# Fixing the order of GpSimd's instructions in the heads' stage of a hybrid attention layer

## The chip, the cores and the metric

The kernel runs on one core of a Trainium2 chip. The metric is device microseconds of one execution. The profile is of one execution apart from the timed ones; its instructions and transfers come from the hardware profiler.

## What is computed

One decoder layer in float32 on 512 tokens of width 2048. Two branches read the same normalised input: sliding-window attention with sinks, and a gated DeltaNet with 16 key heads and 32 value heads of width 128. They are gated, merged and projected. The change touches the DeltaNet branch, whose core is this (cut):

```python
g = jnp.cumsum(g, axis=-1)
decay = jnp.exp(jnp.where(tril, g[..., :, None] - g[..., None, :], -jnp.inf))
...
qk = jnp.where(tril, jnp.einsum('bhncd,bhnsd->bhncs', q, k) * decay, 0.0)
q_dec = q * jnp.exp(g)[..., None]
...
def step(S, xs):
    u_c, w_c, qk_c, qd_c, kd_c, gl_c = xs
    v_new = u_c - w_c @ S
    o = qd_c @ S + qk_c @ v_new
    S = S * gl_c[..., None, None] + jnp.swapaxes(kd_c, -1, -2) @ v_new
    return S, o
```

The layer ends with `y_b = o @ w_o_dn` and a last projection by `w_out`. Both are done by seven products of half-sized blocks each (m1 to m7) in place of eight, for which sums of blocks of the weights are needed.

## The kernel before

Every large product takes three float32r matmuls (L245 to L247): each operand is split into a high part, a cast on ScalarE (`whi`, L52), and a low part, a subtraction on VectorE (`wlo`, L53). Weights come in 1 MB tiles on SyncE's queue (L205).

`deltanet` first makes keys and a triangular inverse, then runs the heads' stage: 16 groups, each with one key head and its two value heads (e = 0, 1). For a group, `heads` runs five channel tiles on TensorE (queries, values 0, values 1, two gates), 48 matmuls each. Beside them, generators (`queries`, `values`, `zgate`, `scan`) are stepped by `pump`, eight times a tile: they issue the small work of this group and the rest of the last one. I call the stretch from a group's sum of squares of queries (L769) to the next group's the segment of that group.

In `queries`, GpSimd and ScalarE work like this for each head:

- `decay_load` (L774) has a row of cumulated gates put on all partitions, into a tile `E`. There are four such tiles, so two groups' worth.
- `decay_mask`, on GpSimd: L781 subtracts the gates of the other axis, L782 (an affine select) masks the upper triangle.
- L926, on ScalarE, takes the exponential; L938, on VectorE, multiplies it with query-key products; the scan's matmul L1004 reads it.
- L932, on GpSimd, multiplies the queries `yq` with decays loaded into `qe`; the scan's L1003 reads that.

In `values`, the convolution goes over ScalarE (L582, `yv`), VectorE (L586, three times), ScalarE again (tanh, L591) and VectorE (L593); TensorE transposes the result (L279, `ptv`) and ScalarE copies it (L882). On VectorE there stand between these: L900 (four columns, for the queries), L1035 and L1042 (output of the group before) and L1051 to L1054 (`head_sums`, sums of its halves, stored by SyncE in L1057). In group 5's segment ScalarE also copies the second inverse out (L836), which SyncE stores (L840).

Beside all this `quad_sums` makes the sums of blocks of `w_od`: a copy from one place of HBM to another (L701, SyncE's queue) and, four steps later, a transfer that adds another block to the copy (L704, GpSimd's queue, 32 of 1 MB). `od_sums` starts in group 2, and each step of `pump` advances it by 0.13 of a copy or transfer. In the attention stage `weight_sums` does the same for `w_out`.

Who goes first on an engine is decided by a scheduler that lists the instructions by when it expects them to be ready; program order counts only where a dependence ties. `behind` adds such ties without a semaphore: what is issued within it is listed after the last matmul so far. The transfers of `od_sums` are issued within it, by `ordered`; the masks, the products with queries and the exponentials of the heads' stage are not.

Of the kernel before, what the change touches and what calls it, by code (L numbers as in the profile page):

```python
# [11 lines left out]
ALU = mybir.AluOpType  # L12
# [4 lines left out]
P = 128  # L17
# [3 lines left out]
NTB = T // P  # L21
# [5 lines left out]
NEG = -1e30  # L27
# [9 lines left out]
class Layer:  # L37
# [66 lines left out]
    @contextmanager  # L104
    def behind(self):

        n, last = len(self.nc.cur_bb.bb.instructions), self.last_mm
        yield
        for i in self.nc.cur_bb.bb.instructions[n:]:
            self.tc.add_manual_dep(  # L110
                i, last.name, mybir.DependencyInfo(mybir.DependencyClass.NoSync, mybir.DependencyReason.DATA),
                reason="behind",
            )

    def step(self, e):
        try:
            e[1] = next(e[0]) or 1
        except StopIteration:
            self.live.remove(e)
# [162 lines left out]
    def build(self):  # L282
        tc, nc, a = self.tc, self.nc, self.a
        with ExitStack() as es:
            self.const = es.enter_context(tc.tile_pool(name="const", bufs=1))
            self.dram = es.enter_context(tc.tile_pool(name="scratch", bufs=1, space=DRAM))
            self.dnc_es = ExitStack()
            self.dnc = self.dnc_es.enter_context(tc.tile_pool(name="dnc", bufs=1, side="right"))
            self.v_d = self.dram.tile([2, P, T], F32, name="v_d")
            self.hpool = es.enter_context(tc.tile_pool(name="h", bufs=1))  # L290
            hh = self.hh = self.hpool.tile([P, KT, T], F32R, name="hh")
            hl = self.hl = self.hpool.tile([P, KT, T], F32R, name="hl")
            self.wraw = es.enter_context(tc.tile_pool(name="wraw", bufs=2, reuse_waits="tile"))
            self.whl = es.enter_context(tc.tile_pool(name="whl", bufs=3, reuse_waits="tile"))
            self.side, self.live, self.slow = {}, [], []
            self.hold, self.keep_order = 0, False
            self.od_d = {n: self.dram.tile([8, P, 2048], F32, name=f"od_{n}") for n in ("m7", "m5", "m6", "m4")}
            self.plan()
            self.psc_es = ExitStack()
            self.psc = self.psc_es.enter_context(tc.tile_pool(name="psc", bufs=4, space=PSUM, reuse_waits="tile"))  # L300
            with ExitStack() as st:
                self.startup(st)
            if self.stop == "startup":
                return
            self.ma_d = self.dram.tile([KT, P, T], F32, name="ma_d")
            self.mb_d = self.dram.tile([KT, P, T], F32, name="mb_d")
            self.ao_d = self.dram.tile([KT, P, T], F32, name="ao_d")
            self.yb_d = self.dram.tile([KT, P, T], F32, name="yb_d")
            self.gate_d = self.dram.tile([D], F32, name="gate_d")
            self.deltanet()  # L310
            self.psc_es.close()
            self.dnc_es.close()
            if self.stop == "deltanet":
                return
            self.y_d = self.dram.tile([KT, P, T], F32, name="y_d")
            self.branch_b()
            if self.stop == "branch_b":
                return
            self.attention()
            if self.stop == "attention":  # L320
                return
            self.finish()
# [369 lines left out]
    def quad_sums(self, q, d, lag):  # L692

        nc = self.nc
        n = len(q(0, 0))
        zip2 = lambda a, b: [x for p in zip(a, b) for x in p]
        copies = zip2(zip(d["m7"], q(1, 0)), zip(d["m5"], q(0, 0))) + list(zip(d["m6"], d["m7"])) + list(zip(d["m4"], d["m6"]))
        adds = zip2(zip(d["m7"], q(1, 1)), zip(d["m5"], q(1, 0))) + list(zip(d["m6"], q(0, 0))) + list(zip(d["m4"], q(0, 1)))
        for i in range(4 * n + lag):
            if i < 4 * n:  # L700
                nc.sync.dma_start(out=copies[i][0], in_=copies[i][1], max_dma_last_dim=8192)  # L701
                yield
            if i >= lag:
                nc.gpsimd.dma_start(out=adds[i - lag][0], in_=adds[i - lag][1], accum_op=ALU.add, max_dma_last_dim=8192)  # L704
                yield

    def weight_sums(self):
# [69 lines left out]
    def decay_mask(self, E, h):  # L777

        nc = self.nc
        ng = self.neg_g[:, :, h].unsqueeze(2).to_broadcast([P, NTB, P])  # L780
        nc.gpsimd.tensor_tensor(out=E, in0=E, in1=ng, op=ALU.add)  # L781
        nc.gpsimd.affine_select(  # L782
            out=E, in_=E, pattern=[[0, NTB], [1, P]], compare_op=ALU.is_ge, fill=NEG, base=0, channel_multiplier=-1
        )

    def solve_load(self, wk, b):
# [98 lines left out]
    def queries(self, wk, g, ps, st):  # L885

        nc = self.nc
        sl = lambda c: slice(c * P, (c + 1) * P)
        q = wk.tile([P, T], F32, tag="y", name="yq", bufs=3)
# [39 lines left out]
        yield 1  # L929
        for e in range(2):  # L930
            qf = qd[e].rearrange("p c i -> p (c i)")
            nc.gpsimd.tensor_tensor(out=qf, in0=qf, in1=q, op=ALU.mult)  # L932
        yield 1
        pqk = self.ptp.tile([P, NTB, P], F32, tag="tp", name="pqk")
        for c in range(NTB):
# [16 lines left out]
        for e in range(2):  # L952
            nc.vector.tensor_tensor(
                out=TT[e][0:HD, :, HD:P],
                in0=pu[e][0:HD],
                in1=self.neg_beta[0:HD, :, 2 * g + e].unsqueeze(2).to_broadcast([HD, NTB, HD]),
                op=ALU.mult,
# [761 lines left out]
```

## Time and profile before

| | |
|---|---|
| median of three timed runs | 2913.67 us (2909.84 to 2913.86) |
| profiled execution | 2902.22 us, its span 2900.5 us |
| TensorE busy | 2833.8 us (98%) |
| VectorE busy | 1863.0 us (64%) |
| ScalarE busy | 1141.2 us (39%) |
| GpSimd busy | 273.9 us (9%), 266 instructions |
| granted TensorE clock | 0.996 on average |
| heads' stage | from about 540 to 1660 us |

A row of the timeline has the start and the length in us, the engine, the line, what is written from what, and in brackets how long the engine stood idle before and what released it. A length includes any time in which the instruction was held up after its start. A row of the table by stage has the stretch, its length, then for TensorE, its weight loads, VectorE, ScalarE and GpSimd the busy time and (x) the instructions, then the granted clock, the share of DMA time and GB/s.

### The profile page before, as it was taken

How to read it: one execution, taken by the hardware profiler on the slowest of the kernel's cores; microseconds unless marked ns; L12 is line 12 of the kernel's file. 1: busy time of each engine (PE TensorE's matmuls, PEld its weight loads, DVE VectorE, ACT ScalarE, POOL GpSimd, SP SyncE). 2: the span in 40 equal slices, each digit the busy share in tenths (PEclk: the TensorE clock that was granted, in tenths of full speed). 3: DMA queues.
4: the chain of work that ended last, by engine and by line, in shares of the span. 5: the costliest groups of instructions: out<-in, count | busy, mean ns of one | idle time of the engine just before them, and what ended most of it. 6: DMA issues, size and time to landing. Idle time of an engine off the chain costs nothing.

```text
span 2900.5 us, 38269 instructions
## 1 busy us (share of the span) xinstructions
PE 2833.8 (98%) x14428; PEld 2322.5 (80%) x14428; DVE 1863.0 (64%) x3020; ACT 1141.2 (39%) x2161; POOL 273.9 (9%) x266
## 2 busy tenths in 40 slices
PE   8899999999999999999999999999999999999999
PEld 6677888888888888787777888888887788788777
DVE  6765998778776656665665456665556655554565
ACT  4355333433334333333333354443344434432343
POOL 0022211101111111111020000000100100000010
PEclk9999999999999999999999999999999999999999
DMA  9757554646667778777782377675745648365575
GB/s 386 288 163 216 161 180 148 203 130 203 204 189 218 235 204 258 227 238 229 226 219 94 133 254 264 241 255 202 223 147 162 171 143 225 112 240 177 182 235 153
DMA packets 205472, 590.08 MB, mean 203 GB/s; under 512 B 74564, under 2 KB 99652, under 8 KB 154088
## 3 DMA queue, kind: packets, MB, share of 16 engines
q1 hardware_dynamic: 195080, 529.44, 53.7%
q0 software_dynamic: 10208, 58.20, 10.2%
q8 instruction: 113, 1.85, 0.3%
q14 instruction: 71, 0.58, 0.1%
HBM read 523.79 MB, written 166.40 MB: 238 GB/s over the span
## 4 chain that ended last, share of the span: by engine, by line
PE 81%; issue 4%; DVE 4%; DMA 2%; POOL 1%; ACT 1%; SPq 0%; POOLq 0%; DVEq 0%; ACTq 0%
PE mm L245 19%; PE mm L247 18%; PE mm L246 18%; PE od L245 4%; PE od L246 4%; PE od L247 4%; PE m L246 1%; PE m L247 1%; PE m L245 1%; PE S L1356 1%; PE pv L985 1%; PE O L1407 1%; PE po L1004 1%; PE pP L279 1%; DVE wlo L53 1%
## 5 line engine op out<-in xcount | busy, mean ns | idle before, releaser
L245 PE MATMUL mm<-hh,whi 128*128 128x512 f32 x2784 | 1134.0, 407 | 2.3 <-ACT whi L52 1.6
L247 PE MATMUL mm<-hh,wlo 128*128 128x512 f32 x2784 | 1090.3, 392 | 1.1 <-DVE wlo L53 1.1
L246 PE MATMUL mm<-hl,whi 128*128 128x512 f32 x2784 | 1088.4, 391 | 0.0
L53 DVE TENSOR_TENSOR wlo<-raw,whi 128x1024 fp32r<-128x1024 f32 (+1 forms) x476 | 587.8, 1238 | 422.7 <-ACT whi L52 414.9
L52 ACT CAST whi<-raw 128x1024 fp32r<-128x1024 f32 (+1 forms) x476 | 495.5, 1044 | 777.8 <-PE mm L246 660.7
L247 PEld LDWEIGHTS mm<-hh,wlo 128*128 128x128 f32 x2784 | 523.2, 188 | 115.4 <-DVE wlo L53 1.9
L245 PEld LDWEIGHTS mm<-hh,whi 128*128 128x128 f32 x2784 | 524.4, 188 | 113.2 <-issue 9.6
L246 PEld LDWEIGHTS mm<-hl,whi 128*128 128x128 f32 x2784 | 524.9, 189 | 99.4 <-issue 1.4
L245 PE MATMUL od<-whi,oh 128*128 128x512 f32 x448 | 174.8, 391 | 0.0
L246 PE MATMUL od<-wlo,oh 128*128 128x512 f32 x448 | 174.4, 389 | 0.0
L247 PE MATMUL od<-whi,ol 128*128 128x512 f32 x448 | 174.4, 389 | 0.0
L932 POOL TENSOR_TENSOR qe<-qe,yq 128x512 f32<-128x512 f32 x32 | 47.2, 1490 | 886.1 <-DMA qe<-eg_rows 575.8
L781 POOL TENSOR_TENSOR E<-E,neg_g 128x512 f32<-128x512 f32 x64 | 84.1, 1316 | 481.4 <-DMA E<-g_rows 362.3
L831 DVE TENSOR_TENSOR A<-A,atmp 128x62 f32<-128x62 f32 (+30 forms) x124 | 112.7, 909 | 1.5
L824 DVE TENSOR_TENSOR atmp<-A 128x62 f32<-128x62 f32 (+30 forms) x124 | 110.2, 888 | 1.4
L247 PEld LDWEIGHTS od<-whi,ol 128*128 128x128 f32 x448 | 84.1, 188 | 17.7
L245 PEld LDWEIGHTS od<-whi,oh 128*128 128x128 f32 x448 | 84.1, 188 | 17.1
L246 PEld LDWEIGHTS od<-wlo,oh 128*128 128x128 f32 x448 | 84.1, 188 | 17.1
L53 DVE TENSOR_TENSOR wlo<-raww,whi 128x1024 fp32r<-128x1024 f32 x56 | 68.3, 1222 | 41.1 <-ACT whi L52 41.1
L52 ACT CAST whi<-raww 128x1024 fp32r<-128x1024 f32 x56 | 59.0, 1055 | 75.4 <-PE m L247 66.2
L978 DVE SCALAR_TENSOR_TENSOR r<-pp,neg_eg,vt 128x128 f32<-128x128 f32 x96 | 29.2, 345 | 78.9 <-PE pp L975 78.5
L1380 ACT ACTIVATE sm<-sm,mx,rs 128x256 f32<-128x256 f32 (+1 forms) x128 | 71.7, 563 | 3.3 <-DVE mx L1375 3.3
(341 smaller groups left out, 3265.7 us busy)
## 6 DMA issues: line engine op xcount, KB each, us to landing
raw<-in_w_ch SPq DMA_DIRECT2D x158, 1024.0 KB
wa<-in_w_ada_ss SPq DMA_DIRECT2D x32, 1024.0 KB
od_m<-in_w_od POOLq DMA_DIRECT2D x32, 1024.0 KB, 14.7
raw<-od_m SPq DMA_DIRECT2D x32, 1024.0 KB
raw<-in_w_od SPq DMA_DIRECT2D x24, 1024.0 KB
E<-g_rows SPq DMA_DIRECT2D x64, 256.0 KB
od_m<-in_w_od SPq DMA_DIRECT2D x16, 1024.0 KB
od_m<-od_m SPq DMA_DIRECT2D x16, 1024.0 KB
```

Of the source, the lines that this page charges most:

```text
L52: self.nc.scalar.copy(out=hi, in_=src)
L53: self.nc.vector.tensor_tensor(out=lo, in0=src, in1=hi.bitcast(F32), op=ALU.subtract)
L245: nc.tensor.matmul(ps, lhsT=wh, rhs=xh, start=first, stop=False)
L246: nc.tensor.matmul(ps, lhsT=wh, rhs=xl, start=False, stop=False)
L247: self.last_mm = nc.tensor.matmul(ps, lhsT=wl, rhs=xh, start=False, stop=last).ins
L279: self.nc.tensor.transpose(dst[:, c * P : (c + 1) * P], src_cols(c), self.ident)
L781: nc.gpsimd.tensor_tensor(out=E, in0=E, in1=ng, op=ALU.add)
L824: eng.tensor_tensor(out=t, in0=A[:, m : m + 1, m + 1 :].to_broadcast([P, m, n]), in1=A[:, :m, m : m + 1].to_broadcast([P, m, n]), op=ALU.mult,
L831: eng.tensor_tensor(out=A[:, :m, m + 1 :], in0=A[:, :m, m + 1 :], in1=t, op=ALU.add)
L932: nc.gpsimd.tensor_tensor(out=qf, in0=qf, in1=q, op=ALU.mult)
L978: nc.vector.scalar_tensor_tensor(out=r[:, e, :], in0=pp[:, e, :], scalar=self.neg_eg[:, c, 2 * g + e : 2 * g + e + 1], in1=v[e][:, c, :], ...
L1380: nc.scalar.activation(t, t, AF.Exp, scale=r[:, h : h + 1], bias=mx[:, h : h + 1], accum_out=den[:, h : h + 1])
```

## The change

A chain of ties is laid through four kinds of instruction on GpSimd: `in_turn` ties each to the one issued before it, without a semaphore. The two steps of `decay_mask`, the adding transfers of `quad_sums` and the products of queries with decays thus stand on GpSimd in the order in which the generators issue them. `keys` and `weight_sums` go through the same functions, but no row moves in their stages. The diff, whole:

```diff
+    def in_turn(self, op):
+
+        if self.turn is not None:
+            self.tc.add_manual_dep(
+                op.ins, self.turn, mybir.DependencyInfo(mybir.DependencyClass.NoSync, mybir.DependencyReason.DATA),
+                reason="in turn",
+            )
+        self.turn = op.ins.name
...
-            self.hold, self.keep_order = 0, False
+            self.hold, self.keep_order, self.turn = 0, False, None
...
             if i >= lag:
-                nc.gpsimd.dma_start(out=adds[i - lag][0], in_=adds[i - lag][1], accum_op=ALU.add, max_dma_last_dim=8192)
+                self.in_turn(
+                    nc.gpsimd.dma_start(out=adds[i - lag][0], in_=adds[i - lag][1], accum_op=ALU.add, max_dma_last_dim=8192)
+                )
                 yield
...
-        nc.gpsimd.tensor_tensor(out=E, in0=E, in1=ng, op=ALU.add)
-        nc.gpsimd.affine_select(
-            out=E, in_=E, pattern=[[0, NTB], [1, P]], compare_op=ALU.is_ge, fill=NEG, base=0, channel_multiplier=-1
+        self.in_turn(nc.gpsimd.tensor_tensor(out=E, in0=E, in1=ng, op=ALU.add))
+        self.in_turn(
+            nc.gpsimd.affine_select(
+                out=E, in_=E, pattern=[[0, NTB], [1, P]], compare_op=ALU.is_ge, fill=NEG, base=0, channel_multiplier=-1
+            )
         )
...
-            nc.gpsimd.tensor_tensor(out=qf, in0=qf, in1=q, op=ALU.mult)
+            self.in_turn(nc.gpsimd.tensor_tensor(out=qf, in0=qf, in1=q, op=ALU.mult))
```

What it moves shows in the engines' rows. First GpSimd in the segment of group 11, before: `qe_11268` and `qe_11274` belong to group 11, the masks `E_11729` and `E_11731` to group 12, `qe_11847` to group 12.

```order
L932 TENSOR_TENSOR qe_11274<-qe_11274,yq_11101 128x512
L781 TENSOR_TENSOR E_11729<-E_11729,neg_g_1305 128x512
L782 AFFINE_SELECT E_11729<-E_11729 128x512
L781 TENSOR_TENSOR E_11731<-E_11731,neg_g_1305 128x512
L782 AFFINE_SELECT E_11731<-E_11731 128x512
L704 DMA od_m6_77<-in_w_od 128x2048 x2
L704 DMA od_m4_78<-in_w_od 128x2048
L932 TENSOR_TENSOR qe_11847<-qe_11847,yq_11681 128x512
```

The same place of the changed kernel (L945 is L932, L792 and L794 are L781 and L782, L714 is L704):

```order
L945 TENSOR_TENSOR qe_11274<-qe_11274,yq_11101 128x512
L714 DMA od_m6_77<-in_w_od 128x2048 x2
L714 DMA od_m4_78<-in_w_od 128x2048
L792 TENSOR_TENSOR E_11729<-E_11729,neg_g_1305 128x512
L794 AFFINE_SELECT E_11729<-E_11729 128x512
L792 TENSOR_TENSOR E_11731<-E_11731,neg_g_1305 128x512
L794 AFFINE_SELECT E_11731<-E_11731 128x512
L945 TENSOR_TENSOR qe_11847<-qe_11847,yq_11681 128x512
```

Three transfers have changed sides with the masks of the next group; this is so, with one to four transfers, for the masks of groups 3 to 14. The masks of groups 0 to 2 and 15 stand as before.

Then ScalarE in the same segment, before: four sums of squares of the queries end, a cast of weights, the first values' convolution `yv_11229`, the exponentials of group 12, another cast, the tanh.

```order
L769 ACTIVATE junk_11190,ss_11183<-ptq_11178 128x128
L52 CAST whi_11301<-raw_11000 128x1024
L582 ACTIVATE yv_11229<-mm_11090,convh_131 128x512
L926 ACTIVATE E_11729<-E_11729 128x512
L926 ACTIVATE E_11731<-E_11731 128x512
L52 CAST whi_11358<-raw_11000 128x1024
L591 ACTIVATE th_11293<-yv_11229 128x512
L882 COPY vt_11333<-ptv_11328 128x512
```

The same place of the changed kernel (L780 is L769, L591 now the convolution that was L582, L600 the tanh that was L591, L895 is L882):

```order
L780 ACTIVATE junk_11190,ss_11183<-ptq_11178 128x128
L52 CAST whi_11301<-raw_11000 128x1024
L591 ACTIVATE yv_11229<-mm_11090,convh_131 128x512
L52 CAST whi_11358<-raw_11000 128x1024
L600 ACTIVATE th_11293<-yv_11229 128x512
L895 COPY vt_11333<-ptv_11328 128x512
```

The exponentials of group 12 are gone from here. They now stand in the next segment, that of group 12 itself, on ScalarE of the changed kernel (L939 is L926):

```order
L780 ACTIVATE junk_11769,ss_11762<-ptq_11757 128x128
L52 CAST whi_11880<-raw_11580 128x1024
L591 ACTIVATE yv_11809<-mm_11670,convh_131 128x512
L939 ACTIVATE E_11729<-E_11729 128x512
L939 ACTIVATE E_11731<-E_11731 128x512
L52 CAST whi_11938<-raw_11580 128x1024
L600 ACTIVATE th_11872<-yv_11809 128x512
```

Before, the exponentials at this place were those of group 13. Other groups' exponentials moved likewise, mostly to a place just ahead of their own group's sums of squares. TensorE's and SyncE's rows are the same in both kernels; on VectorE L900 and one L53 change places with two L586 once, in one segment.

## The prediction

> **What bounds the kernel now.** I read the page's busy times first, then busy time by stage, then what TensorE waited for.
>
> ```profile
> span 2900.5 us, 38269 instructions
> PE 2833.8 (98%) x14428; PEld 2322.5 (80%) x14428; DVE 1863.0 (64%) x3020; ACT 1141.2 (39%) x2161; POOL 273.9 (9%) x266
> ...
> 690.00:1520.00 830.00, 814.41 (x4276) 676.01 (x4274) 538.25 (x909) 309.97 (x682) 112.80 (x106) 0.99 0.75 224
> 1990.00:2560.00 570.00, 569.37 (x3152) 457.67 (x3150) 333.22 (x649) 230.71 (x481) 40.12 (x34) 1.00 0.56 172
> ```
>
> TensorE is the bound: 98% busy, and in attention (the last row) it lacks 0.6 of 570 us, so time won earlier is not lost there again. The heads' stage, the only one in which rows move, leaves 15.6 of 830 us idle at a granted clock of 0.99. This is all that the change can win, besides the clock. TensorE's timeline, cut to the idle times over a microsecond (in brackets, with the releaser), tells what they are:
>
> ```profile
> 926.90 1.22 PE L1000 MATMUL pd<-vs,k 128*128 128x256 f32 x2 [2.37 <-DVE vs L992]
> 1169.12 1.08 PE L279 MATMUL ptv<-ident,yv 128*128 128x128 f32 x4 [2.65 <-DVE yv L593]
> 1240.02 0.63 PE L279 MATMUL ptv<-ident,yv 128*128 128x128 f32 x4 [1.86 <-DVE yv L593]
> 1310.50 0.63 PE L279 MATMUL ptv<-ident,yv 128*128 128x128 f32 x4 [2.98 <-DVE yv L593]
> 1380.90 1.09 PE L279 MATMUL ptv<-ident,yv 128*128 128x128 f32 x4 [2.89 <-DVE yv L593]
> 1451.63 0.63 PE L279 MATMUL ptv<-ident,yv 128*128 128x128 f32 x4 [1.74 <-DVE yv L593]
> 1522.06 0.63 PE L279 MATMUL ptv<-ident,yv 128*128 128x128 f32 x4 [2.98 <-DVE yv L593]
> ```
>
> Six times, once a group from group 9 to 14, the first values' transposition (L279) waits for VectorE's L593, which needs ScalarE's tanh (L591). Here is group 11 (1310.50) on ScalarE, GpSimd and VectorE:
>
> ```profile
> 1298.18 0.69 ACT L582 ACTIVATE yv<-mm,convh 128x512 f32<-128x512 f32 x1
> 1304.80 0.63 ACT L926 ACTIVATE E<-E 128x512 f32<-128x512 f32 x1 [5.93 <-POOL E L782]
> 1306.60 0.63 ACT L926 ACTIVATE E<-E 128x512 f32<-128x512 f32 x1 [1.16 <-POOL E L782]
> 1307.13 1.03 ACT L52 CAST whi<-raw 128x1024 fp32r<-128x1024 f32 x1
> 1308.07 0.62 ACT L591 ACTIVATE th<-yv 128x512 f32<-128x512 f32 x1
> ```
> ```profile
> 1299.03 3.03 POOL L932 TENSOR_TENSOR qe<-qe,yq 128x512 f32<-128x512 f32 x2 [59.53 <-DMA qe<-eg_rows]
> 1302.03 2.03 POOL L781 TENSOR_TENSOR E<-E,neg_g 128x512 f32<-128x512 f32 x1
> 1304.13 0.64 POOL L782 TENSOR_SCALAR_AFFINE_SELECT E<-E 128x512 f32<-128x512 f32 x1
> 1304.74 1.05 POOL L781 TENSOR_TENSOR E<-E,neg_g 128x512 f32<-128x512 f32 x1
> ...
> 1306.51 2.53 POOL L704 DMA_DIRECT2D od_m<-in_w_od  x3
> ```
> ```profile
> 1299.58 1.25 DVE L900 TENSOR_SCALAR epsq<-ss 128x4 f32<-128x4 f32 x1
> 1301.41 1.74 DVE L53 TENSOR_TENSOR wlo<-raw,whi 128x1024 fp32r<-128x1024 f32 x1
> ...
> 1304.98 1.08 DVE L1053 TENSOR_TENSOR osb<-zh 128x256 f32<-128x256 f32 x1
> ...
> 1308.19 1.23 DVE L53 TENSOR_TENSOR wlo<-raw,whi 128x1024 fp32r<-128x1024 f32 x1 [1.52 <-ACT whi L52]
> 1309.34 0.42 DVE L1051 TENSOR_TENSOR osb<-zh 128x256 f32<-128x256 f32 x1
> 1309.67 0.68 DVE L593 SCALAR_TENSOR_TENSOR yv<-th,yv 128x512 f32<-128x512 f32 x1
> ```
>
> Two things make L593 late. ScalarE sits in front of the mask exponentials (L926, for the next group) until GpSimd has masked; its cast (L52) and tanh are queued behind, and VectorE idles 1.52 us for the cast. And VectorE is itself stretched where GpSimd computes: L900, on four columns, took 1.25 us beside the query products; L1053 took 1.08 against 0.42 for its like L1051. While the three transfers ran (1306.51 to 1309.04), L53 took 1.23, its undisturbed time. So I read: a computing GpSimd instruction and a VectorE one with operands in SBUF exclude each other, whole instructions in turn; issuing a transfer excludes nothing.
>
> **The change, part by part.** It adds and removes no instruction. TensorE's and SyncE's rows do not move, VectorE's in one harmless place, so all rests on two moves.
>
> *First: GpSimd's transfers go ahead of the masks.* Group 11's masks begin three transfers (2.53 us) later, other groups' one to four. Behind them stand the next query products, some 60 us away. A transfer waits for its copy, which now holds up the masks; the closest case is the last one:
>
> ```profile
> 1435.07 0.52 SPq L701 DMA_DIRECT2D od_m<-od_m  x1
> 1448.19 1.55 POOL L932 TENSOR_TENSOR qe<-qe,yq 128x512 f32<-128x512 f32 x1 [0.68 <-DMA qe<-eg_rows]
> ```
>
> That copy would have some 17 us to land (four transfers follow 1449.7). If it needs more, group 14's masks slip, whose exponentials now come some 50 us later. I cost this at nothing; uncovered it would be those few microseconds once.
>
> ```profile
> L704 POOL DMA_DIRECT2D od_m<-in_w_od x32: 823/1112/2053, 691.9 to 1455.9; - x32
> ```
>
> [...]
>
> *Second: the exponentials leave their place behind the first values' convolution* in the segments of groups 2 to 13 and go 25 to 42 rows later, when the mask has long been made. ScalarE's wait for it goes:
>
> ```profile
> ACT E L926 <- POOL E L782: 84.9, 26, 7.1
> ```
>
> Group 14's segment keeps its order (mask 15, no transfer left), so the wait at 1522.06 stays as a control. In segments 7 and 12 the place is kept, but what stands there are the exponentials of that group itself, masked a group's time before. Their 2 x 0.63 us per group fall in new places in which ScalarE idles for TensorE anyway; if it did not, they would cost at most 1.3 us.
>
> **What is late next** is VectorE's own chain, so the waits don't simply vanish. I replayed each group: instructions at their undisturbed times, GpSimd and VectorE excluding each other, each going when its turn comes. For the old order this gives 2.69, 1.93, 3.02, 2.93, 1.95 and 3.02 us for the six waits, against 2.65, 1.86, 2.98, 2.89, 1.74 and 2.98 in the rows. In the new order, group 11: products until 1302.06, transfers until 1304.6, first mask sum until 1305.64; L1053 waits for it and ends at 1306.0; L1042 until 1306.6; then the second mask sum goes first (until 1307.48), L53 until 1308.6, the second selection (0.64) until 1309.2, L1051 until 1309.5, L593 until 1310.1: TensorE waits 2.73. The masks have moved onto the very instructions ahead of L593. Likewise 2.14 (group 9), 1.97 (10), 1.96 (12), 0.99 (13; four transfers push the masks past L593), 3.02 (14). **Won: 0.55 - 0.04 + 0.29 + 0.97 + 0.96 = 2.7 us.** Bounds: 12.1 if no mask met VectorE's chain (2.65 + 1.86 + 2.98 + 2.89 + 1.74); the loss is the slower rival below.
>
> *The wait at 926.90* comes by a longer chain; first VectorE's row in group 5, then the chain of work in order of time:
>
> ```profile
> 890.67 1.79 DVE L593 SCALAR_TENSOR_TENSOR yv<-th,yv 128x512 f32<-128x512 f32 x1 [2.55 <-ACT th L591]
> ```
> ```profile
> 895.89 0.35 DVE osb L1054
> 896.26 19.65 DMA oq_d<-osb
> 915.99 6.09 DMA ta_d<-atmp
> 922.11 0.31 ACT atmp L836
> ```
>
> The tanh of group 5 also stood behind an exponential, and VectorE idled 2.55 us for it. Without that, less a mask collision on the way (0.66, as L1053's 1.08 against 0.42), L1054 comes up to 1.9 us sooner, and three transfers no longer start just ahead of that store. I take **1.7 us**, between 0 (the store lands when it did) and 2.37.
>
> *The clock.* Stretches of 3.4 us behind some of the waits:
>
> ```profile
> 926.60:930.00 3.40, 3.10 (x11) 2.88 (x12) 1.45 (x5) 2.01 (x3) 0.00 (x0) 0.52 0.60 77
> 1169.00:1172.40 3.40, 3.28 (x10) 2.82 (x11) 1.93 (x3) 0.61 (x2) 0.00 (x0) 0.51 0.95 211
> 1380.80:1384.20 3.40, 3.30 (x10) 2.85 (x11) 1.91 (x3) 0.63 (x2) 0.00 (x0) 0.51 1.01 226
> 1522.00:1525.40 3.40, 3.34 (x21) 2.88 (x21) 2.31 (x4) 2.11 (x3) 0.00 (x0) 1.00 0.90 314
> ```
>
> Three waits (2.37, 2.65, 2.89) were followed by half the clock: 10 or 11 matmuls instead of 21, 1.7 us lost each. Two of 2.98 were not, nor any below 2.3. So of five waits over 2.3 us three were punished, 0.6 each. The replay leaves two (2.73, 3.02), and 2.14 near the edge: 1.2 to 1.5 halvings instead of 3. **Won: 1.5 x 1.7 = 2.6 us**, between 0 and 5.1.
>
> [...]
>
> **Sum:** 2.7 + 1.7 + 2.6 = 7.0 us of the profiled execution's 2902.22 (span 2900.5 and 1.7 around it), 0.24%. The median, 2913.67, is 11.5 us above that execution, for reasons outside this stage; I take the same 7.0 off it: **2906.7**.
>
> **Rivals.** *No change (within 0.2%, 5.8 us, about what a measurement of this kernel can tell from no change).* ScalarE's wait was only cover: VectorE, met by the later masks, is just as late. The replay's 2.7 us is all: 2911.0. For it: in group 10 the replay wins nothing. [...] Against it: group 11 loses a VectorE wait of 1.52 us that shows in a row.
>
> *Slower.* The masks, moved by 1.7 to 2.5 us, fall in full on L1051 and L593: a mask sum and a selection (1.04 + 0.64 us) ahead of L593 in five groups, 8.4 us, and every wait then exceeds 2.3, so two more halvings, 3.4 us; 2913.67 + 11.8 = 2925.5. It decides if the query products begin about a microsecond later against VectorE's chain than in these rows. Against it: ScalarE's wait is gone by then, which gives back what VectorE idled for the cast, 1.52 us in group 11.
>
> *The change does not do what it says* is excluded by the rows of the order; it could only move nothing that matters, which is the first rival.
>
> **How the numbers follow.** Faster by over 0.2%: 0.52 (the forecast lies just beyond, and best is 12.1 + 2.4 + 5.1 = 19.6 us, 2894). Within: 0.38. Slower: 0.10. The range reaches down to 2897 (16.7 of those 19.6 us) and up to 2916 (a loss of 2.3), which leaves out most of the slower case and the last of the gains, some 0.15 together. The likeliest case's own range is 2897 to 2908.
>
> **What would show it.** ScalarE's waits no longer name GpSimd's L782 beyond some 20 us (groups 0 to 2 and 15's mask); the wait near 1522 stays near 3 us; the ones of groups 9 to 13 shrink by what is listed, not to nothing; the halved stretches drop to one or two; 926.90 falls under a microsecond. Wrong would be: waits of groups 9 to 13 unchanged or longer with L1051 or L593 stretched (the slower case), all gone (my exclusion rule is too strict), or new TensorE waits in groups 2 to 8.

## The result and the profile after

| | before | after |
|---|---|---|
| first comparison, medians of five runs | 2913.36 us | 2898.47 us, ratio 0.9951 (0.9937 to 0.9966) |
| second comparison, medians of 17 and 6 runs | 2911.85 us | 2901.73 us, ratio 0.9963 (0.9950 to 0.9977) |
| profiled executions, two each: span | 2900.5, 2908.3 us | 2894.2, 2900.0 us |

(Intervals hold 95%.) Faster by 0.4 to 0.5%, 10 to 15 us, where 7.0 was forecast; 2898.47 lies in the range, 1.5 us from its lower end. The direction is right and so is the place. The size is not, and of the two reasons given for one of the waits only one holds. This is the first profile of the changed kernel, page and heads' stage:

```profile
span 2894.2 us, 38268 instructions
PE 2832.6 (98%) x14428; PEld 2322.2 (80%) x14428; DVE 1872.6 (65%) x3020; ACT 1138.7 (39%) x2161; POOL 278.9 (10%) x266
...
690.00:1520.00 830.00, 818.58 (x4314) 679.94 (x4313) 556.72 (x919) 310.90 (x685) 120.63 (x108) 1.00 0.76 226
```

TensorE's idle time in the stretch fell from 15.6 to 11.4 us, while VectorE became *busier*: over the whole execution, with the same 3020 instructions, 1863.0 to 1872.6 us, so some are held up for longer. (In the stretch alone, 538.25 to 556.72, ten more instructions are counted, which may explain a part.) What TensorE waits for now (L288 is L279, L602 is L593, L963 and L959 are L950 and L946):

```profile
1107.12 0.27 PE L963 MATMUL pu<-tt,Y 64*64 64x64 f32 x1 [1.39 <-DVE Y L959]
1167.95 0.95 PE L288 MATMUL ptv<-ident,yv 128*128 128x128 f32 x4 [2.38 <-DVE yv L602]
1238.85 0.63 PE L288 MATMUL ptv<-ident,yv 128*128 128x128 f32 x4 [1.85 <-DVE yv L602]
1307.79 0.63 PE L288 MATMUL ptv<-ident,yv 128*128 128x128 f32 x4 [1.44 <-DVE yv L602]
1377.02 0.63 PE L288 MATMUL ptv<-ident,yv 128*128 128x128 f32 x4 [1.73 <-DVE yv L602]
1514.42 0.63 PE L288 MATMUL ptv<-ident,yv 128*128 128x128 f32 x4 [2.64 <-DVE yv L602]
```

The wait that was at 926.90 is gone, and so is group 13's. The five others are there still, and a new one (1107.12) has come, which the second profile has not. ScalarE's row on the masks:

```profile
ACT E L939 <- POOL E L794: 20.0, 6, 5.5
```

That is 20.0 us in 6 waits, where it was 84.9 in 26. And group 11, whose wait went from 2.98 to 1.44, on ScalarE, GpSimd and VectorE (L600 is the tanh, L1064 is L1051):

```profile
1301.61 1.05 ACT L52 CAST whi<-raw 128x1024 fp32r<-128x1024 f32 x1 [3.92 <-PE mm L255]
1302.56 0.63 ACT L600 ACTIVATE th<-yv 128x512 f32<-128x512 f32 x1
```
```profile
1299.49 3.27 POOL L945 TENSOR_TENSOR qe<-qe,yq 128x512 f32<-128x512 f32 x2 [60.29 <-DVE yv L595]
1302.72 2.52 POOL L714 DMA_DIRECT2D od_m<-in_w_od  x3
1304.35 1.96 POOL L792 TENSOR_TENSOR E<-E,neg_g 128x512 f32<-128x512 f32 x1
1306.39 0.71 POOL L794 TENSOR_SCALAR_AFFINE_SELECT E<-E 128x512 f32<-128x512 f32 x1
```
```profile
1303.58 1.52 DVE L53 TENSOR_TENSOR wlo<-raw,whi 128x1024 fp32r<-128x1024 f32 x1
1305.02 1.59 DVE L1064 TENSOR_TENSOR osb<-zh 128x256 f32<-128x256 f32 x1
1306.53 1.11 DVE L602 SCALAR_TENSOR_TENSOR yv<-th,yv 128x512 f32<-128x512 f32 x1
```

The cast and the tanh run 5.5 us earlier than before (1.2 of them won in earlier groups), and L53 no longer waits for the cast. But the masks, now behind three transfers, fall on L1064 (1.59 for 0.42) and L602 (1.11 for 0.68). So far this is the forecast's picture. What stood open was how much each half of the change does, why the timed runs won twice what two profiles showed, and what the clock takes.

### The profile page after: what moved, and what is told of

Same layout as the page of the kernel before. It is cut to its first block, busy times and chain, and to the rows that moved or that the text cites. A ratio compares the mean times of both kernels' runs of the same rounds, so it can differ in the third digit from the quotient of the medians.

```text
span 2894.2 us, 38268 instructions
## 1 busy us (share of the span) xinstructions
PE 2832.6 (98%) x14428; PEld 2322.2 (80%) x14428; DVE 1872.6 (65%) x3020; ACT 1138.7 (39%) x2161; POOL 278.9 (10%) x266
## 3 DMA queue, kind: packets, MB, share of 16 engines
q8 instruction: 113, 1.85, 0.3%
## 4 chain that ended last, share of the span: by engine, by line
PE 82%; DVE 4%; issue 4%; DMA 2%; ACT 1%; POOL 0%; SPq 0%; DVEq 0%; POOLq 0%; ACTq 0%
PE mm L254 19%; PE mm L256 19%; PE mm L255 19%; PE od L255 3%; PE od L254 3%; PE od L256 3%; PE m L255 1%; PE m L256 1%; PE m L254 1%; PE S L1369 1%; DVE wlo L53 1%; PE pv L998 1%; PE po L1017 1%; PE pP L288 1%; PE O L1420 1%
## 5 line engine op out<-in xcount | busy, mean ns | idle before, releaser
L53 DVE TENSOR_TENSOR wlo<-raw,whi 128x1024 fp32r<-128x1024 f32 (+1 forms) x476 | 591.7, 1246 | 412.7 <-ACT whi L52 403.2
L945 POOL TENSOR_TENSOR qe<-qe,yq 128x512 f32<-128x512 f32 x32 | 51.0, 1614 | 873.0 <-DMA qe<-eg_rows 504.3
L792 POOL TENSOR_TENSOR E<-E,neg_g 128x512 f32<-128x512 f32 x64 | 87.0, 1359 | 479.1 <-DMA E<-g_rows 332.7
L53 DVE TENSOR_TENSOR wlo<-raww,whi 128x1024 fp32r<-128x1024 f32 x56 | 68.3, 1222 | 41.1 <-ACT whi L52 41.1
```

The costliest lines, as they stand in the source:

```text
L53: self.nc.vector.tensor_tensor(out=lo, in0=src, in1=hi.bitcast(F32), op=ALU.subtract)
L792: self.in_turn(nc.gpsimd.tensor_tensor(out=E, in0=E, in1=ng, op=ALU.add))
L945: self.in_turn(nc.gpsimd.tensor_tensor(out=qf, in0=qf, in1=q, op=ALU.mult))
```

## The experiments

The theory: ScalarE's wait for the masks (84.9 us in 26 waits before), with the cast and the tanh queued behind it, was the cost; what remains is GpSimd and VectorE excluding each other (L602 above took 1.11 us for 0.68); a long wait is punished by the clock (three of the five over 2.3 us before, 1.7 us each). Rivals: the transfers' place helped, or VectorE's own chain is late anyway.

**Before and after, once more.**

> The kernel before, unchanged, profiled and timed a second time. It asks how far one profiled execution speaks for the timed ones, because the change won 6.3 us between two profiled spans (2900.5 to 2894.2) and 14.9 us between the medians. If the first profile of before was a quick execution, the new span lies some 5 to 11 us higher (2905 to 2912), while TensorE's waits at the first values' transposition in groups 9 to 14 are the same within 0.3 us (2.65, 1.86, 2.98, 2.89, 1.74, 2.98), and the difference is in halved stretches of the clock (each 1.7 us) or outside the heads' stage. Rival: the waits of the heads' stage themselves differ from one execution to the next, and the 11 us lie there. Timed ratio 1.000 within 0.002.

> The changed kernel, unchanged, a second time. If its profile speaks for it, the waits at the first values' transposition are again 2.38, 1.85, 1.44, 1.73, under 0.3 and 2.64 us (groups 9 to 14) within 0.3 us, the wait that was at 926.90 is again gone, the new one at L963 near 1107 (1.39 us) is there again, and the number of halved stretches in the heads' stage is 0 to 2. Timed ratio 0.994 to 0.997, as in the first comparison. Rival: the change is worth only what the two profiled spans differ by, 6.3 us, ratio 0.998.

Measured: the second executions' ratios are 0.9999 (0.9990 to 1.0008) for before against itself and 0.9963 for after. The new profile of before has a span of 2908.3 us, 7.8 more than the first. The waits are the same within 0.3 us, but for 3.05 near 927, group 14's 2.63 and group 11's:

```profile
1312.64 1.08 PE L279 MATMUL ptv<-ident,yv 128*128 128x128 f32 x4 [3.49 <-DVE yv L593]
...
1167.90:1171.30 3.40, 0.76 (x6) 0.58 (x6) 2.83 (x5) 1.04 (x2) 0.54 (x1) 1.00 0.87 296
1171.30:1174.70 3.40, 3.40 (x12) 2.82 (x11) 1.40 (x3) 1.77 (x3) 0.00 (x0) 0.50 1.08 223
```

The last two rows are a window with a wait (0.76 us busy of 3.40) and the next one, at half the clock. The first profile has six such halved windows of 3.41 us (not counting the one that ends the execution), three of them in the heads' stage; this one has eleven, five there. Five windows at 1.7 us are 8.5 us. The first execution was a lucky one: it is the only profiled one that is not among the timed runs, and its 2902.22 us are less than every timed run of before took (2905.61 at least). After's two have six and eight, one and two of them in the stage. Its waits stay within 0.1 us, except in groups 11 (2.30 for 1.44), 13 (0.74 for none) and 14 (2.96 for 2.64), and the one at 1107, which is gone.

**ScalarE's half alone.**

> One half of the change alone: GpSimd's rows stand as in the kernel before (masks ahead of the transfers), but the mask exponentials on ScalarE are tied behind the last matmul at their place in the program, so they come after the group's own first tanh, 60 us after their masks, in every group from 0 to 15. Theory (ScalarE's wait for the mask is what made the first values late): the replay with whole instructions of GpSimd and VectorE excluding each other gives waits of 2.04, 1.93, 1.47, 1.34, 1.95, 1.47 us in groups 9 to 14, 10.2 in all against 14.1 before; the control wait of group 14 shrinks too, because its exponentials go as well; none is over 2.3, so at most one halved stretch is left in the heads' stage. With the wait at 926.90 gone: a span of 2888 to 2894 and a timed ratio of 0.994 to 0.997, the same as the changed kernel or better. Rival (the transfers' place ahead of the masks is what helped): the waits stay at 14 us and the ratio is 0.999 to 1.001.

```diff
-        for e in range(2):
-            nc.scalar.activation(M[e], M[e], AF.Exp)
+        with self.behind():
+            [nc.scalar.activation(M[e], M[e], AF.Exp) for e in range(2)]
```

Measured: 2896.64 us, 0.9952 (0.9936 to 0.9968): as fast as the whole change, without a row of GpSimd moved. No wait of ScalarE for L782 is left in the stage. TensorE's waits:

```profile
927.37 0.70 PE L1000 MATMUL pd<-vs,k 128*128 128x256 f32 x2 [3.14 <-DVE vs L992]
1168.28 0.63 PE L279 MATMUL ptv<-ident,yv 128*128 128x128 f32 x4 [1.34 <-DVE yv L593]
...
1306.15 0.63 PE L279 MATMUL ptv<-ident,yv 128*128 128x128 f32 x4 [1.06 <-DVE yv L593]
1374.76 0.63 PE L279 MATMUL ptv<-ident,yv 128*128 128x128 f32 x4 [1.11 <-DVE yv L593]
1510.91 0.63 PE L279 MATMUL ptv<-ident,yv 128*128 128x128 f32 x4 [1.34 <-DVE yv L593]
```

Groups 9 to 14 together: 6.7 us, against 15.1 before and 10.0 and 11.8 after (the replay: 10.2). The control of group 14, 2.98, is 1.34 now that its exponentials went too. So ScalarE's wait was the cost. Groups 9 to 13, whose exponentials go late in both kernels, wait 5.4 us here and 7.4 and 8.9 in the changed kernel: there the transfers' place ahead of the masks gives part of the gain back. What failed is the wait near 927: it should have gone with the tanh's delay, and is longer. Two halved windows are left in the stage, one of them there, where one at most was expected. The chain of waits says why:

```profile
894.71 21.17 DMA oq_d<-osb
...
915.96 6.64 DMA ta_d<-atmp
```

The store starts 1.55 us sooner than before (894.71 for 896.26) and the chain goes on at 915.9 all the same.

**GpSimd's work held back.**

> The changed kernel, and besides GpSimd's products with queries and its masks wait for ScalarE's copy of the first values' transposition of their segment, so that no computing GpSimd instruction runs while VectorE works towards L593. Theory (what is left of the waits is GpSimd and VectorE excluding each other): the replay without GpSimd gives no wait in any of groups 9 to 14, all under 0.3 us, and no halved stretch in the heads' stage: against the changed kernel 10.0 us of waits and one halving of 1.7 less, a span near 2883 and a timed ratio of 0.990 to 0.993. Rival one: what is left is VectorE's own chain, then the waits stay at some 10 us and the ratio at 0.995. Rival two: the moved products and masks hit the second values or the inverse's rows (L959, L966), and new TensorE waits of 1 to 2 us a group appear some 5 to 14 us later; then the ratio is 0.995 or above.

```diff
+    def after_values(self, op):
+        if self.vmark is not None:
+            self.tc.add_manual_dep(
+                op.ins, self.vmark, mybir.DependencyInfo(mybir.DependencyClass.Sync, mybir.DependencyReason.DATA),
+                reason="after values",
+            )
+        return op
...
+        vc = nc.scalar.copy(out=vt.rearrange("p c d -> p (c d)"), in_=pt)
+        if e == 0:
+            self.vmark = vc.ins.name
...
-        self.in_turn(nc.gpsimd.tensor_tensor(out=E, in0=E, in1=ng, op=ALU.add))
+        self.in_turn(self.after_values(nc.gpsimd.tensor_tensor(out=E, in0=E, in1=ng, op=ALU.add)))
...
-            self.in_turn(nc.gpsimd.tensor_tensor(out=qf, in0=qf, in1=q, op=ALU.mult))
+            self.in_turn(self.after_values(nc.gpsimd.tensor_tensor(out=qf, in0=qf, in1=q, op=ALU.mult)))
```

(`vmark` is the copy of the first values' transposition. The products also stand later in `queries`, behind L938's.) Measured: 2884.66 us, 0.9908 (0.9893 to 0.9923), span 2882.5. No wait of groups 9 to 14 is left. The stage, and group 11 on VectorE (L1075 is L1051, L611 is L593) and GpSimd (L963):

```profile
690.00:1520.00 830.00, 827.52 (x4380) 687.65 (x4379) 532.76 (x926) 312.10 (x688) 106.92 (x110) 1.00 0.76 227
```
```profile
1298.56 1.22 DVE L53 TENSOR_TENSOR wlo<-raw,whi 128x1024 fp32r<-128x1024 f32 x1
1299.69 0.42 DVE L1075 TENSOR_TENSOR osb<-zh 128x256 f32<-128x256 f32 x1
1300.03 0.68 DVE L611 SCALAR_TENSOR_TENSOR yv<-th,yv 128x512 f32<-128x512 f32 x1
```
```profile
1302.94 2.53 POOL L963 TENSOR_TENSOR qe<-qe,yq 128x512 f32<-128x512 f32 x2 [58.91 <-ACT vt L904]
```

TensorE is busy 827.5 of 830 us, and the three VectorE rows take their undisturbed times (1.22, 0.42 and 0.68 us). VectorE's own chain was never late: both rivals fall. Only the wait near 927 is back (2.48 us, and a halved window). Group 11's L593 took 0.68 us here, 1.11 under a mask in the changed kernel and 1.53 under one in the kernel with late exponentials alone.

**Only the masks held back.**

> The changed kernel, and besides only the masks wait for ScalarE's copy of the first values' transposition; the products with queries stay where they are, ahead of it. The two groups of GpSimd work are told apart: the replay without masks gives waits of 1.50, 0.83, 0.83, 0.82, 0.99 and 0.83 us in groups 9 to 14 (5.8 in all, against 10 to 12 in the changed kernel and 0 in the one with both held back). Theory (each of both holds VectorE): a sum of 4 to 7 us, no halved stretch there, ratio to before 0.992 to 0.995. Rival (the masks alone are it): waits under 0.3 us, ratio 0.991, as with both held back. Other rival (the products alone): waits as in the changed kernel, ratio 0.996.

The edit is the same without its last replaced line. Measured: 2889.78 us, 0.9925 (0.9907 to 0.9942); groups 9 to 14 wait 5.4 us in all (0.67, 0.68, 1.28, 0.68, 0.86, 1.25). So masks and products share what remains about equally, as the replay had it (5.8), and the wait near 927 is absent. One halved window is left in the stage, near 1574, at a later wait of 2.24 us; none was expected.

**No adding transfers.**

> The kernel with late exponentials and GpSimd's old order, from which the 32 adding transfers of the sums of w_od are left out, so that the last product gets copies in place of sums. Two questions. The wait near 927, 3.14 us there although the tanh of group 5 no longer stands behind an exponential: if it hangs on what the DMA engines have to do when the inverse's rows are stored (their share was 1.04 until 920 with three adding transfers just before, and fell at 910 to 915 in the changed kernel, which has two there), it goes, under 0.3 us; if it hangs on VectorE's rows before the store, it stays at 2.4 to 3.2. And the waits of groups 9 to 14 (1.34, 1.85, 1.06, 1.11, 0, 1.34): if issuing a transfer excludes nothing, they stay within 0.3 us, but for group 10, where a transfer stands between the masks; if it holds VectorE, they fall below 0.6.

Measured, in one execution: span 2889.1 us. The wait near 927 is gone; those of groups 9 to 14 are 1.78, 1.32, 1.26, 1.79, none and 1.79, so not one falls below 0.6. But three waits grew by 0.4 to 0.7, more than the 0.3 allowed; that the two engines' turns fell otherwise is argued, not shown. Rows settle better whether issuing a transfer holds VectorE. In seven profiles (before and after, both twice, late exponentials, masks held back, masks and products held back), between 690 and 1520 us, L53 and L593 beside nothing but the issue of a transfer took 1.21 to 1.23 us (16 rows) and 0.68 to 0.69 (14 rows), as they do undisturbed; beside a computing GpSimd instruction they took up to 2.31 and 2.66.

**A pause in group 5**, with GpSimd held back, and with late exponentials only.

> The kernel with GpSimd's work held back, and besides no copy or transfer of the sums of w_od is issued during group 5, in whose segment the inverse's rows are stored; from group 6 on they run at 0.14 of one a step in place of 0.13. Theory (the wait near 927, 2.48 us and halved, comes from the DMA engines' load): it goes, and the span falls by 2.5 to 4.2 us from 2882.5, to 2878 to 2880; ratio to before 0.988 to 0.990. Rival: the wait stays, or the denser transfers later make another wait of 1 to 3 us; then the ratio stays at 0.991.

> Late exponentials with GpSimd's old order of masks and transfers, and no copy or transfer of the sums of w_od issued during group 5 (from group 6 on at 0.14 a step in place of 0.13); nothing is left out. If the wait near 927 hangs on the DMA engines' load while the inverse's rows are stored, it goes (3.14 us there with the same order of GpSimd and no pause), and the span falls from 2892.7 by 3 to 5 us, to 2888 to 2890, ratio to before 0.992 to 0.994: better than the changed kernel (0.995 and 0.996) without its order on GpSimd. If it hangs on anything else, it stays at 2.4 to 3.2 and the ratio at 0.995. The waits of groups 9 to 14 stay between 1.0 and 2.0 us each, or are under 0.3 where the products' loads come late (group 13).

```diff
+                    if g in (5, 6):
+                        self.side["ws"][0][1] = 0.0 if g == 5 else 0.14
                     self.heads(wk, g)
```

Measured: in both kernels the wait near 927 is gone, though two transfers still fall between 885 and 905, where there were three. The first takes 2882.96 us, 0.9900 (0.9884 to 0.9916), the lowest median of all, though its interval overlaps that of the kernel without the pause; in its stage one wait over 0.25 us is left (1.30). Its span, 2880.9, is only 1.6 us shorter for the 2.5 to 4.2 expected, as one more window is halved (7 for 6), none of them in the stage. The second takes 2894.61, 0.9943 (0.9927 to 0.9960), less than hoped: its waits of groups 9 to 14 grew to 11.3 us. Group 12 shows it, on GpSimd (L934 and L783 are L932 and L781) and VectorE (L1053 is L1051):

```profile
1367.71 1.30 POOL L934 TENSOR_TENSOR qe<-qe,yq 128x512 f32<-128x512 f32 x1 [0.48 <-DMA qe<-eg_rows]
1368.97 3.22 POOL L783 TENSOR_TENSOR E<-E,neg_g 128x512 f32<-128x512 f32 x2
```
```profile
1367.83 2.27 DVE L53 TENSOR_TENSOR wlo<-raw,whi 128x1024 fp32r<-128x1024 f32 x1
1370.02 1.27 DVE L1053 TENSOR_TENSOR osb<-zh 128x256 f32<-128x256 f32 x1
1371.22 1.53 DVE L593 SCALAR_TENSOR_TENSOR yv<-th,yv 128x512 f32<-128x512 f32 x1
```

The second product waited for its load. So the masks began 2.1 us before TensorE was due at its transposition (1371.07), where the kernel without the pause has 5.5 us (1368.15 and 1373.65), and they hit L53, L1053 and L593 in full. That is the slower rival of the forecast, in small: products that end some 3 us later decide it.

**The price of a wait.** A first try added waits that did not take hold.

> What a wait of TensorE costs beyond itself. To the kernel with GpSimd's work held back, in which TensorE hardly waits in the heads' stage, 32 waits of known places are added: in each of the two gate tiles of a group TensorE waits for four VectorE instructions on a scratch tile (256 to 640 columns) that themselves wait for the matmul before; waits of 1.5 to 3.5 us. Theory, from the waits and halved stretches of six profiles: the clock is halved for the next window when over about 2.15 us of one window of a fixed 3.41 us grid are idle; so no wait below 2.1 us is followed by a halved stretch, of those of 2.3 to 2.7 us some 40 to 50 in 100, of those from 3.0 to 3.5 some 60 to 75, and each costs 1.7 us more. Rival one (a wait has to fill a window of 3.41 us): no halved stretch at all, or only after the longest. Rival two (the length alone decides, with no grid): all above some length, none below.

Later matmuls were listed ahead of the waiting one; the waits were 0.6 us at most and nothing was halved, so it tells nothing. The second one ties them behind:

> What a wait of TensorE costs beyond itself, with the added waits now really in its way (in the run before, matmuls that came later had been listed ahead of the waiting one, and the waits were 0.6 us at most). In each of the 32 gate tiles of the heads' stage TensorE waits for four VectorE instructions on a scratch tile (320 to 640 columns), and the 17 matmuls of the product after it are tied behind; waits of some 1.7 to 3.3 us, some longer or in pieces where small products of the scan stand between. The rule taken from the nine profiles so far: the clock is halved after a window of a fixed 3.41 us grid when over 2.1 us of that window are idle, wherever the wait began; it parts all 53 waits over 1.2 us of those profiles (13 halved, 40 not) with one offset between the two clocks. If the rule holds, the same offset and 2.1 us part the new waits, with at most 2 of 32 wrong; waits below 2.1 us are never punished, and of those from 2.3 to 3.3 us half to three quarters are. Rival one (a wait has to fill a window of 3.41 us): none of those under 3.4 us is. Rival two (the length alone decides, with no grid): one length parts them as well.

```diff
+        for i in range(4):
+            op = self.nc.vector.tensor_tensor(out=t, in0=t, in1=t, op=ALU.max).ins
+            if i == 0:
+                self.tc.add_manual_dep(op, self.last_mm.name, d, reason="stall")
+        self.stalled, self.pinned = (op.name, d), 6
```

Measured: span 2982.7 us, 15 halved windows in the stage. The waits that came are up to 2.2 us long. Rival one falls: none fills a window, 15 are punished. Rival two falls as well: a wait of 2.18 us that lies across two windows is not punished, and one of 1.18 is (with 0.50 idle just before it):

```profile
571.55 0.50 PE L264 MATMUL mm<-hh,whi 128*128 128x512 f32 x1 [1.18 <-DVE idle L284]
795.32 0.70 PE L1050 MATMUL pd<-vs,k 128*128 128x256 f32 x2 [2.18 <-DVE vs L1042]
```
```profile
569.00:572.40 3.40, 1.72 (x10) 1.23 (x9) 3.02 (x9) 0.96 (x2) 0.00 (x0) 1.00 1.03 358
572.40:575.80 3.40, 3.40 (x10) 2.66 (x9) 0.78 (x1) 0.00 (x0) 0.00 (x0) 0.50 0.18 47
790.90:794.30 3.40, 1.78 (x11) 1.17 (x9) 3.40 (x6) 0.96 (x2) 0.00 (x0) 1.00 1.02 209
794.30:797.70 3.40, 2.28 (x10) 1.59 (x11) 3.28 (x8) 1.01 (x5) 0.00 (x0) 1.00 1.04 293
```

But the forecast of at most 2 wrong failed: 8 halved windows come after less than 2.1 us of idle time. Windows, counted with all idle time in them, tell more than waits: in the ten other profiles 15 windows of the stage at full clock have 1.95 us or more of their 3.41 idle, and all 15 are followed by half the clock; 49 have 1.0 to 1.94 idle, and none is. Here the 8 above 1.95 are punished too, but also 7 of the 11 between 1.6 and 1.94. Small products of the scan stand in all of these 11 windows; what exactly the clock weighs there is left open.

## Why the prediction was right or wrong

One account holds for the ten profiles of the eight kernels without added waits: the span, less TensorE's waits over 0.25 us from 540 to 1700, less 1.7 us for each halved window of the execution, leaves the same.

| kernel | span | waits | of them groups 9 to 14 | halved windows (in the stage) | rest |
|---|---|---|---|---|---|
| before, first and second | 2900.5, 2908.3 | 21.6, 22.3 | 15.1, 15.1 | 6 (3), 11 (5) | 2868.7, 2867.3 |
| after, first and second | 2894.2, 2900.0 | 15.5, 16.0 | 10.0, 11.8 | 6 (1), 8 (2) | 2868.5, 2870.4 |
| exponentials late | 2892.7 | 13.3 | 6.7 | 7 (2) | 2867.5 |
| the same, no adds | 2889.1 | 11.4 | 7.9 | 5 (0) | 2869.2 |
| the same, pause | 2895.4 | 14.9 | 11.3 | 7 (2) | 2868.6 |
| masks held back | 2889.1 | 9.3 | 5.4 | 5 (1) | 2871.3 |
| masks and products held back | 2882.5 | 3.8 | none | 6 (1) | 2868.5 |
| the same, pause | 2880.9 | 1.3 | none | 7 (0) | 2867.7 |

- *The bound* (TensorE, only its waits in the heads' stage count): right; the spans differ by 27 us and the rest by 4.
- *ScalarE's wait for the mask makes L593 late:* right, shown by the late exponentials alone. The row fell to 20.0 us, as said, and the control, group 14, kept its wait (2.64 and 2.96 after, 2.98 and 2.63 before).
- *GpSimd and VectorE exclude each other, issuing a transfer excludes nothing:* right as far as the rows go. With GpSimd's work held back, the waits of groups 9 to 14 (10.0 and 11.8 us) went; beside a computing GpSimd instruction L593 took up to 2.66 us, beside the issue of transfers 0.68 to 0.69. L1042, which reads PSUM, was not held up: 0.67 to 0.69 us beside a computing GpSimd instruction, in 17 rows each of before and after. That whole instructions go in turn was the author's reading; by it the replay came within 0.21 us of each of the six waits of before. After the change the replay's six waits add up to 12.8 us; 10.0 and 11.8 were measured. Single ones were off by up to 1.3 (group 11: 2.73 for 1.44 and 2.30): there L53 went ahead of the first mask sum, which the replay had the other way round. The term, 2.7 us, was 5.1 and 3.3.
- *The transfers hold up the masks by their own time (2.53 us in group 11):* by no more. The three took 2.52 us, and the first mask sum began 1.63 us after their start; single ones took 0.82 to 1.76 us, where one took 2.05 before.
- *The wait at 926.90* went, 2.37 us (3.05 in the second profile) for the forecast's 1.7, but **the first of its two reasons was wrong**: "Without that ... L1054 comes up to 1.9 us sooner" does not shorten it. The late exponentials brought the store forward by 1.55 us and the wait stayed, at 3.14; in the changed kernel the store starts later than before (897.88 for 896.26) and the wait is gone. The second reason, "three transfers no longer start just ahead of that store", fits: the wait hangs on what the DMA engines have to do, and they are full until 920 before, and not after. Here is before, 910 to 920, and then after:

```profile
910.00:915.00 5.00, 5.00 (x27) 4.25 (x26) 2.67 (x9) 3.54 (x6) 0.00 (x0) 1.00 1.06 370
915.00:920.00 5.00, 5.00 (x25) 4.16 (x24) 2.23 (x4) 1.45 (x6) 0.00 (x0) 1.00 1.04 356
```
```profile
910.00:915.00 5.00, 5.00 (x26) 4.18 (x25) 3.61 (x10) 3.17 (x5) 0.00 (x0) 1.00 0.84 288
915.00:920.00 5.00, 5.00 (x26) 4.18 (x25) 1.65 (x2) 4.96 (x10) 0.00 (x0) 1.00 0.41 75
```

  The share (the last number but one) drops 5 us sooner. What is slowed is the next pair of transfers, the inverse's rows that ScalarE's L836 must see stored before it can go on. On SyncE's queue, before and then after (L853 is L840):

```profile
915.99 1.39 SPq L840 DMA_DIRECT2D ta_d<-atmp  x2
923.25 1.46 SPq L840 DMA_DIRECT2D ta_d<-atmp  x2
```
```profile
915.48 1.47 SPq L853 DMA_DIRECT2D ta_d<-atmp  x2
919.48 1.44 SPq L853 DMA_DIRECT2D ta_d<-atmp  x2
```

  The second pair follows after 7.3 us, and after 4.0. All ten profiles part so: the four with the wait have three adding transfers issued between 885 and 905 and 7.3 to 9.9 us between the pairs, the six without it two transfers or none, and 4.0. Without the adds, or with the pause, the wait goes in the old order too. The bound named for this term ("the store lands when it did") was what happened in the experiment.
- *The clock:* that some waits are followed by 3.41 us at half the clock is right, 1.7 us each, and 0.6 for each wait above 2.3 is near what was seen (12 of 18 in the ten profiles), but the term was mis-sized, because it started from the three halvings of one execution. Two executions of before have 3 and 5 in the stage, of after 1 and 2: 2.5 fewer on average, 4.3 us for 2.6. Windows with 1.95 to 2.8 us of their 3.41 idle were enough, and the length of a wait alone does not decide: near 927 one of 2.37 us was followed by half the clock in the first execution of before, and one of 3.05 in the second was not.
- *"11.5 us above that execution, for reasons outside this stage"* is the other step that **failed**, in part. The second profile of before lies 7.8 us above the first with five more halved windows, and two of these are in the stage. Waits and halvings of the stage cost 26.7 and 30.8 us before, 17.2 and 19.4 after: 10.4 us on average, close to the second comparison's 10.1 and inside the first one's interval (9.9 to 18.4). The first one's 14.9 needs no cause of its own, as the two intervals overlap (the second is 6.7 to 14.6).
- *The sum:* by the means of the two profiles each, the three terms, forecast at 2.7, 1.7 and 2.6 us, came out at 4.2, 2.7 and 4.3, and other waits took 0.7 back. All three were too small; none made up for another.
- *No new waits:* wrong once. At 1107.12 the later masks held L1065 (L1052 before) and L53, and the inverse's product waited 1.39 us; the second profile has 0.2.

Of the rivals, "VectorE is just as late" holds for groups 9 and 10 of the change (2.38 for 2.65, 1.85 for 1.86); the slower one did not come true, though the pause shows its mechanism. Transfers ahead of the masks with the exponentials left early was not tried, so what that half does alone is known only from the comparison of groups 9 to 13.

## What to carry to other kernels

Where an engine waits with other work listed behind, as ScalarE did with a cast and the tanh (5.93 us in group 11 before), ask first whether what it waits for is needed there: a tie that lists the instruction later was worth as much as the whole reordering (ratio 0.9952, against 0.9951 and 0.9963), and it moved no row of GpSimd. Where GpSimd computes, look for VectorE instructions longer than their like beside it (here L593, up to 2.66 us for 0.68), and hold GpSimd back until the chain that TensorE waits for is through (ratio 0.9908 here). And before a difference of a few us is read off two profiles, profile the same kernel twice (7.8 us apart here).

## What the runs showed of the hardware

- The granted clock changes on a fixed 3.41 us grid: in each profile the halved stretches, but for the one that ends the execution, last 3.41 or 6.83 us and begin multiples of 3.41 us apart. In ten profiles, when TensorE was idle for 1.95 us or more of one (57%), the next ran at half clock, 15 of 15 times; with 1.0 to 1.94, none of 49. This is no general limit: with the added waits, 7 of 11 windows with 1.6 to 1.94 us idle were punished too. A wait of 2.0 to 3.1 us costs nothing more, or 1.7 us, by where it falls on the grid: one of 3.05 us (second profile of before, split 1.90 and 1.15) went unpunished, one of 1.95 (late exponentials with the pause) did not. Two waits of the stage (2.96 and 3.49 us) cost two windows: a halved window with 0.87 or 1.41 us idle was followed by another, while the 15 with 0.27 or less were followed by the full clock.
- Two profiles of one kernel differed by five such windows, and by 7.8 us of 2900 in the span. The timed runs of before scatter by 12.1 us (2905.6 to 2917.7).
- A store started 1.55 us sooner ended no sooner (21.17 us for 19.65), while the DMA engines were full (share 0.98 to 1.06 from 905 to 920 us in both profiles). One adding transfer of 1 MB more, three for two, went with 7.3 to 9.9 us in place of 4.0 between two pairs of small stores some 10 to 25 us later.
- A VectorE instruction of 0.68 us (L593) took up to 2.66 beside a computing GpSimd instruction, and 0.68 to 0.69 beside the issue of transfers.
